# An attention phase that hands its transfers to another engine's queue: half-row tiles, block sums as tasks of their own, and a second bank for the last products

## The chip, the cores and the metric

The kernel runs on one core of a Trainium2 chip. The metric is the device time of one execution in microseconds. Each engine of the core (TensorE, written PE in the profile; VectorE, DVE; ScalarE, ACT; GpSimd, POOL; SyncE, SP) works through its own list of instructions in the order in which the program recorded them, and waits at an instruction until the semaphores that it needs have come. PE's weight loads stand in rows of their own (PEld). SP computes nothing and issues transfers; ACT computes and can issue transfers too. A row whose engine is written SPq or ACTq is such an issue.

## The reference

One decoder layer on x, 2048 rows of 1024 numbers in float32. Three groups of heads share one input projection; their outputs are normalized, projected, and added to x; a feed-forward part with squared ReLU follows.

```python
h = rms_norm(x, norm1_g)
proj = einsum('bld,de->ble', h, w_in)
o_a = swa_sink_mixer(...)      # window attention, 256 columns
o_b = s5_mixer(...)            # state space, 512 columns
o_c = nsa_mixer(...)           # compressed, selected and window attention, 256 columns
mixed = concatenate([rms_norm(o_a, g), rms_norm(o_b, g), rms_norm(o_c, g)])
x = x + einsum('ble,ed->bld', mixed, w_out)
h2 = rms_norm(x, norm2_g)
hid = relu(einsum('bld,df->blf', h2, w_up))
x = x + einsum('blf,fd->bld', hid * hid, w_down)
```

## The kernel before

The rows of x are cut into 16 tiles of 128. A float32 product is made of three products: each operand is split into a high part and the rest (`split`, L1766 and L1767: a cast on ACT, a subtraction on DVE), and high·high, high·low and low·high are summed in one PSUM bank. Phases follow each other: the front (input projection), a stretch that merges window attention, the gated output of the state space and compression, `phase_mix` (about 600 to 1280 us), `phase_up` and `phase_down`.

`phase_mix` holds the third attention, the output projection and the residual. It is written as generators, one for each piece of a tile's work, that yield an engine with an estimated duration, an event, or a ring (a set of buffers). A planner, `Flow`, takes at each step the task that can start first by these estimates, with ties broken by rank, and so fixes one order for each engine when the program is built. On the chip each engine follows that order, whatever the true durations are.

For the output projection of tile i these tasks follow each other:

- `opening`: once for the phase, raw rows of `w_out` are loaded on SP, 128 × 1024 at a time (oraw, L1161), and split into wo_h on ACT (L1168) and wo_l on DVE (L1169).
- `front`: projected queries and keys are loaded on SP (tc, L1192 and L1193).
- `closing`: the attention's output is stored on SP (oc_d, L1579).
- `finished`: the three groups' outputs are loaded on SP (mix, L1595 to L1597) and scaled on POOL (L1604); the third group is squared on ACT (sq, L1608), normalized on POOL (L40 to L45, then L1610). PE transposes (ptx, L1622, in the single bank "pt"), and ACT and DVE split the result into mh (L1624) and ml (L1625), in two halves.
- `filled`: the tile of x is loaded on SP (mx, L1638); then 2 × 24 products (pw, L1657), the first half of the columns before the second, in the single bank "pw". The last tile is an exception: its two halves alternate, and the second uses the bank "pt". Below, pw131 is tile 13's second half.
- `added`: DVE adds pw to mx (L1672), ACT squares the sum into the bank (L1673). Only then is the bank free.
- `posted`: both halves together are stored as x1 on ACT (L1682). For tiles 0 to 7, POOL scales the row (L1689), PE transposes it (pth, L1697), ACT copies (L1701), SP stores it as hT (L1703). At its end, for tiles 7 to 14, one eighth of the block sums is made: four loads of hT on SP (mt, L1715), four subtractions on POOL (L1719), four stores on SP (sums, L1720).

Raw rows of `w_out`, rows of x and block sums share one ring of two 128 × 1024 buffers, "xt". Logits use the two banks of "pq".

`phase_up` multiplies by a scheme of seven products in the order 1, 6, 7, 5, 2, 4, 3. Its factors come from hT (1, 2, 3) and from the block sums (4, 5, 6, 7): each is loaded on SP (fx, L1852) and split into fh (ACT, L1766) and fl (DVE, L1767). The weights' factors are loaded on SP (ur, L1879), partly combined on POOL (fs, L1891), and split into uh and ul. The products (pua to pud) are L1920. Its first loads and splits are recorded among the last work of `phase_mix`.

```python
for i in range(NT):
    spawn(front(i), 100 * i + R_FRONT, 0.0)
    spawn(compressed(i), 100 * i + R_CMP, 0.0)
    spawn(attended(i), 100 * i, 0.0)
    spawn(finished(i), 100 * i + R_FINISH, 0.0)
```

Of the kernel before, what the change touches and what calls it, by code (L numbers as in the profile page):

```python
# [1082 lines left out]
def phase_mix(tc, C, x, gains, B, cmp, w_out, out_norm_g, g2, pd, oa_d, ob, x1, hT, xs, rr, rh, ss_a, ss_b, r_d, oc_d, release):  # L1083
# [4 lines left out]
    with ExitStack() as ctx:  # L1088
# [17 lines left out]
        for t in (kBw[64:96].bitcast(F32), q_lo[0][64:96].bitcast(F32), q_lo[1][64:96].bitcast(F32), slc):  # L1106
# [9 lines left out]
                                     ("qd", 1), ("tc", 1), ("xt", 2), ("mix", 1), ("mh0", 1), ("mh1", 1), ("fill", 1), ("oc", 2))}  # L1116
# [3 lines left out]
        wout = [Event() for _ in range(NK)]  # L1120
# [30 lines left out]
        def opening():  # L1151
# [3 lines left out]
            for k in range(NK):  # L1155
                yield R["xt"]
                box = {}

                def load(k=k):
                    box["r"] = late["fp"].tile([P, D], F32, tag="xt", name=f"oraw{k}", bufs=2)  # L1160
                    nc.sync.dma_start(box["r"], w_out[0, k * P:(k + 1) * P])  # L1161
                t = yield "SP", 50, load
                landed = Event()
                fire(landed, t + DMA_NS + 2600)
                yield landed
                for n in range(2):
                    sl = slice(512 * n, 512 * n + 512)
                    yield "ACT", 714, lambda: nc.scalar.activation(late["wh"][k][:, sl], box["r"][:, sl], AF.Copy, scale=late["go"][:, k:k + 1])  # L1168
                    t = yield "DVE", 796, lambda: nc.vector.scalar_tensor_tensor(late["wl"][k][:, sl], box["r"][:, sl], late["go"][:, k:k + 1],  # L1169
                                                                                 late["wh"][k][:, sl], op0=ALU.mult, op1=ALU.subtract)  # L1170
                put(R["xt"], t)
                fire(wout[k], t)
                if k == 3:
                    yield R["pw"]
                    yield "PE", 60, turn_rows
                    t = yield "DVE", 300, lambda: nc.vector.tensor_copy(late["rb"], late["ptr"])
                    put(R["pw"], t)
# [6 lines left out]
        def front(i):  # L1184
# [5 lines left out]
            def load():  # L1190
                S["tc"] = lp.tile([P, 524], F32, tag="tc", name=f"tc{i}", bufs=1)
                nc.sync.dma_start(S["tc"][:, 0:256], pd["b"][i * P:i * P + P, 128:384])  # L1192
                nc.sync.dma_start(S["tc"][:, 256:524], pd["c"][i * P:i * P + P, 128:396])  # L1193
            t = yield "SP", 100, load
# [365 lines left out]
        def closing(i, exps, fin, den, w, b, po, prev, done, logits_done, nm_, end, rank):  # L1560
# [17 lines left out]
            if end:  # L1578
                t = yield "SP", 50, lambda: nc.sync.dma_start(oc_d[i * P:i * P + P], S["oc"].rearrange("p h d -> p (h d)"))  # L1579
# [3 lines left out]
        def finished(i):  # L1583
# [9 lines left out]
            def load():  # L1593
                mix = box["mix"] = fp.tile([P, D], F32, tag="mix", name=f"mix{i}", bufs=1)
                nc.sync.dma_start(mix[:, 0:256], oa_d[rows])  # L1595
                nc.sync.dma_start(mix[:, 256:768], ob[rows])
                nc.sync.dma_start(mix[:, 768:D], oc_d[rows])  # L1597
            t = yield "SP", 150, load
            yield landing(t, 5e5)
            mix = box["mix"]  # L1600
            if i == 0:
                yield wout[4]
# [29 lines left out]
        def filled(i, mh, ml):  # L1632
            wh, wl = late["wh"], late["wl"]
            yield R["fill"]
            yield R["xt"]
            rows = slice(i * P, i * P + P)
            xt_ = late["fp"].tile([P, D], F32, tag="xt", name=f"mx{i}", bufs=2)
            t = yield "SP", 50, lambda: nc.sync.dma_start(xt_, x[0, rows])  # L1638
            landed, outs = landing(t, 5e5), [Event(), Event()]
            spawn(posted(i, xt_, outs, rows), 100 * i + R_FINISH, 0.0)  # L1640
            order = [(n, k) for n in range(2) for k in range(NK)]
            if i == NT - 1:
                order = [(n, k) for k in range(NK) for n in range(2)]
            pw = {}
            for n, k in order:
                sl = slice(512 * n, 512 * n + 512)
                if i < 2:
                    yield wout[k]
# [661 lines left out]
```

## Time and profile before

| | |
|---|---|
| median of 3 runs | 2544.19 us (2543.75 to 2546.55) |
| profiled execution, its own time | 2548.41 us |
| its span in the trace | 2546.6 us |
| mean granted clock of TensorE in it | 0.984 of full speed |
| PE busy | 96% of the span |
| DVE, ACT, POOL busy | 70%, 52%, 40% |

The span is cut into 40 slices of 63.7 us on the page. Each digit is the busy share of an engine in a slice, in tenths; PEclk is the granted clock. The edited phase holds slices 10 to 20 and the start of 21, counted from 1. How PE's waits lie within these slices is read from the trace's rows: each has its start, its duration, the engine and source line, output and inputs by the program's names, and in brackets the idle time of the engine just before it with what ended that.

### The profile page before, as it was taken

The page shows a single profiled execution, that of the slowest core. Times are in us where ns is not written, and L with a number is a line of the kernel's source. Part 1 is how long each engine was busy: PE and PEld are TensorE (multiplying, and loading weights), DVE is VectorE, ACT ScalarE, POOL GpSimd, SP SyncE. Part 2 cuts the span into 40 slices and gives each one's busy share as a digit, 9 for nine tenths or more (in the row PEclk, how much of TensorE's full clock was granted, in tenths as well). Part 3 has the DMA queues.
Part 4 walks back from the last instruction along what each step waited for, and adds up shares of the span by engine and source line. Part 5 has one row for each costly group of instructions (what it writes and reads, how often), then busy time and mean ns, then how long its engine had stood idle before and what let it go on. Part 6 is the DMA issues. An engine that isn't in the chain of part 4 may idle for free. (4 is left out here: it accounts for less than half of the span.)

```text
span 2546.6 us, 37996 instructions
## 1 busy us (share of the span) xinstructions
PE 2440.5 (96%) x12766; PEld 2071.8 (81%) x12766; DVE 1771.2 (70%) x3496; ACT 1325.9 (52%) x2768; POOL 1021.1 (40%) x1015
## 2 busy tenths in 40 slices
PE   8999998999799999999799999999999999999999
PEld 7799997777578888888578878788887888888887
DVE  7853876754687788888355555755558888888886
ACT  6453546754576667666255554544444444334442
POOL 0000222211243333332646665566555444545447
PEclk9999999999899999999899999999999999999999
DMA  7462335221222122222466667755547534444335
GB/s 234 136 204 83 106 95 169 80 60 42 80 84 84 59 69 75 65 80 77 146 216 186 188 193 220 220 152 153 152 122 262 160 103 125 135 131 132 121 101 196
DMA packets 394867, 337.21 MB, mean 132 GB/s; under 512 B 42758, under 2 KB 357772, under 8 KB 393232
## 3 DMA queue, kind: packets, MB, share of 16 engines
q1 hardware_dynamic: 357488, 308.56, 40.2%
q10 hardware_dynamic: 37184, 26.22, 3.2%
q8 instruction: 101, 1.65, 0.3%
q14 instruction: 94, 0.77, 0.1%
HBM read 220.15 MB, written 114.55 MB: 131 GB/s over the span
## 5 line engine op out<-in xcount | busy, mean ns | idle before, releaser
L1766 ACT CAST v<-vr 128x512 fp32r<-128x512 f32 x224 | 139.4, 624 | 304.7 <-DMA vr<-vd 144.2
L1767 DVE TENSOR_TENSOR v<-vr,v 128x512 fp32r<-128x512 f32 x224 | 233.6, 1051 | 78.8 <-ACT v L1766 78.6
L2099 PE MATMUL pdc<-dw,v 128*128 128x512 f32 x768 | 187.4, 393 | 4.0 <-ACT dw L1766 2.9
L2099 PE MATMUL pdb<-dw,v 128*128 128x512 f32 x768 | 184.7, 389 | 0.0
L2099 PE MATMUL pda<-dw,v 128*128 128x512 f32 x768 | 184.5, 389 | 0.0
L2099 PEld LDWEIGHTS pdc<-dw,v 128*128 128x128 f32 x768 | 145.3, 190 | 35.5 <-ACT dw L1766 3.4
L2099 PEld LDWEIGHTS pdb<-dw,v 128*128 128x128 f32 x768 | 144.5, 188 | 30.1
L2099 PEld LDWEIGHTS pda<-dw,v 128*128 128x128 f32 x768 | 144.1, 188 | 30.0
L546 POOL TENSOR_TENSOR t<-Q,E 128x508 f32<-128x508 f32 x16 | 22.0, 1376 | 362.9 <-ACT Q L526 324.7
L1766 ACT CAST uh<-fs 128x512 fp32r<-128x512 f32 x124 | 76.2, 621 | 157.2 <-PE pub L1920 58.9
L1891 POOL TENSOR_TENSOR fs<-ur,ur 128x512 f32<-128x512 f32 x62 | 87.3, 1408 | 166.6 <-DMA ur<-in_w_up 120.0
L1767 DVE TENSOR_TENSOR ul<-fs,uh 128x512 fp32r<-128x512 f32 x124 | 124.3, 1004 | 35.1 <-ACT uh L1766 34.9
L1767 DVE TENSOR_TENSOR ul<-ur,uh 128x512 fp32r<-128x512 f32 x93 | 93.5, 1007 | 50.1 <-ACT uh L1766 46.8
L1657 PE MATMUL pw<-wo_h,mh 128*128 128x512 f32 x256 | 104.8, 409 | 16.5 <-ACT pw L1673 15.5
L1337 ACT CAST ths<-pps 128x512 fp32r<-128x512 f32 (+1 forms) x144 | 79.0, 563 | 69.8 <-PE pps L1321 62.5
L1936 POOL TENSOR_TENSOR ev<-e,e 128x512 f32<-128x512 f32 x64 | 93.3, 1458 | 49.1 <-issue 24.7
L1920 PE MATMUL puc<-fh,uh 128*128 128x512 f32 x256 | 101.8, 398 | 6.7 <-ACT fh L1766 3.4
L1342 DVE TENSOR_TENSOR tls<-pps,ths 128x512 fp32r<-128x512 f32 (+1 forms) x144 | 92.5, 657 | 21.4 <-ACT ths L1337 20.2
L1920 PE MATMUL pub<-fh,uh 128*128 128x512 f32 x256 | 102.8, 402 | 2.4 <-DVE e L1929 2.4
L1657 PE MATMUL pw<-wo_h,ml 128*128 128x512 f32 x256 | 104.4, 408 | 0.0
L1657 PE MATMUL pw<-wo_l,mh 128*128 128x512 f32 x256 | 104.1, 407 | 0.0
L1920 PE MATMUL pub<-fl,uh 128*128 128x512 f32 x256 | 102.1, 399 | 0.0
(563 smaller groups left out, 7814.7 us busy)
## 6 DMA issues: line engine op xcount, KB each, us to landing
vr<-vd SPq DMA_DIRECT2D x224, 256.0 KB
vd<-ev SPq DMA_DIRECT2D x128, 256.0 KB
ur<-in_w_up SPq DMA_DIRECT2D x124, 256.0 KB
vd<-e ACTq DMA_DIRECT2D x64, 256.0 KB
dr<-in_w_down SPq DMA_DIRECT2D x32, 512.0 KB
x<-in_x SPq DMA_DIRECT2D x16, 512.0 KB
mx<-in_x SPq DMA_DIRECT2D x16, 512.0 KB
x<-mx ACTq DMA_DIRECT2D x16, 512.0 KB
```

The lines of the kernel that those rows point to most:

```text
L546: nc.gpsimd.tensor_tensor(t[:, :, :, 0:n], Q[:, :, :, 0:n], e.rearrange("p g j c -> p j g c")[:, :, :, 0:n], op=ALU.mult)
L1337: yield "ACT", cast_ns(n), lambda: nc.scalar.copy(th[:, 0:nb], pt[:, 0:nb])
L1342: t = yield "DVE", sub_ns(n), lambda: nc.vector.tensor_tensor(tl[:, 0:nb], pt[:, 0:nb], th[:, 0:nb], op=ALU.subtract)
L1657: t = yield "PE", mm_ns(512), lambda: nc.tensor.matmul(pw[n], a[half][:, j], b[k][:, sl], start=k == 0 and m == 0, stop=k == NK - 1 and m ...
L1766: nc.scalar.copy(dh, src)
L1767: nc.vector.tensor_tensor(dl, src, dh, op=ALU.subtract)
L1891: nc.gpsimd.tensor_tensor(t, x, y, op=op)
L1920: nc.tensor.matmul(bank[b], w[:, k], h[o][:, k], start=first and k == 0 and n == 0, stop=k == HALF - 1 and n == 2, skip_group_check=True)
L1936: nc.gpsimd.tensor_tensor(tile_("v" + o), x, y, op=op)
L2099: nc.tensor.matmul(bank[b, q], x[:, q, j], y[:, j], start=first and j == 0 and n == 0, stop=j == 1 and n == 2, skip_group_check=True)
```

## The change

All of it is in `phase_mix`; `phase_up` is as it was, with its line numbers 17 higher.

1. The loads of tc, of raw `w_out`, of mix and of x, and the store of oc_d are issued by ACT instead of SP.
2. The "xt" ring is four buffers of 128 × 512 instead of two of 128 × 1024. Raw rows of `w_out` and rows of x come in halves. x1 is stored half by half. The splitting of a half of the weights is a task of its own (`weighed`), as is the transposition of the norms (`rows_turned`); tiles 0 and 1 wait for each half of a weight row by itself.
3. Block sums are eight tasks of their own (`block_sums`), each started once hT of tiles m and m + 4 is stored, where m is 0 to 3.
4. For tiles 14 and 15 the second half of the products uses a bank of "pq"; tile 15's halves follow each other like the other tiles'.

```diff
-                                     ("qd", 1), ("tc", 1), ("xt", 2), ("mix", 1), ...
+                                     ("qd", 1), ("tc", 1), ("xt", 4), ("mix", 1), ...
-        wout = [Event() for _ in range(NK)]
+        wout = {(k, n): Event() for k in range(NK) for n in range(2)}
+        rows_there = Event()
...
             for k in range(NK):
-                yield R["xt"]
-                    box["r"] = late["fp"].tile([P, D], F32, tag="xt", name=f"oraw{k}", bufs=2)
-                    nc.sync.dma_start(box["r"], w_out[0, k * P:(k + 1) * P])
...
                 for n in range(2):
                     sl = slice(512 * n, 512 * n + 512)
+                    yield R["xt"]
+                    raw = late["fp"].tile([P, 512], F32, tag="xt", name=f"oraw{k}{n}", bufs=4)
+                    t = yield "ACT", 60, lambda: nc.scalar.dma_start(raw, w_out[0, k * P:(k + 1) * P, sl])
+                    spawn(weighed(k, n, raw, sl), 60 + k, t)
                 if k == 3:
+                    spawn(rows_turned(), 60, t)
...
-                nc.sync.dma_start(S["tc"][:, 0:256], pd["b"][i * P:i * P + P, 128:384])
+                nc.scalar.dma_start(S["tc"][:, 0:256], pd["b"][i * P:i * P + P, 128:384])
...
-                t = yield "SP", 50, lambda: nc.sync.dma_start(oc_d[i * P:i * P + P], ...)
+                t = yield "ACT", 60, lambda: nc.scalar.dma_start(oc_d[i * P:i * P + P], ...)
...
-                nc.sync.dma_start(mix[:, 0:256], oa_d[rows])
+                nc.scalar.dma_start(mix[:, 0:256], oa_d[rows])
...
-            order = [(n, k) for n in range(2) for k in range(NK)]
-            if i == NT - 1:
-                order = [(n, k) for k in range(NK) for n in range(2)]
+            spawn(loaded(i, rows, xh, landed), 100 * i + R_FINISH - 2, 0.0)
+            order = [(n, k) for n in range(2) for k in range(NK)]
...
-                    alt = i == NT - 1 and n
-                    yield R["pt"] if alt else R["pw"]
-                    p, tag = (ps_t, "pt") if alt else (late["ps"], "pw")
+                    alt = i >= ENDING and n
+                    yield R["pq"] if alt else R["pw"]
+                    p, tag, bufs = (ps_s, "pq", 2) if alt else (late["ps"], "pw", 1)
...
+        def loaded(i, rows, xh, landed):
+            for n in range(2):
+                yield R["xt"]
+                xh[n] = late["fp"].tile([P, 512], F32, tag="xt", name=f"mx{i}{n}", bufs=4)
+                t = yield "ACT", 60, lambda: nc.scalar.dma_start(xh[n], x[0, rows, 512 * n:512 * n + 512])
...
-            yield "ACT", 60, lambda: nc.scalar.dma_start(x1[rows], xt)
+                t = yield "ACT", 60, lambda: nc.scalar.dma_start(x1[rows, 512 * n:512 * n + 512], xh[n])
...
+        def block_sums(m, half):
+            yield E[m]["hT"]
+            yield E[m + 4]["hT"]
...
+            for m in range(4):
+                for half in range(2):
+                    spawn(block_sums(m, half), 100 * (m + 4) + 450, 0.0)
```

What this moves is seen in the order of the engines' instructions. First ACT at the end of the phase, from the last cast of an up weight (uh0153) on; mh140 and mh141 are the halves of tile 14's transposed rows, pw130 and pw131 the squares that free tile 13's bank. Before:

```order
L1766 CAST uh0153_16049<-fs0154_16043 128x512
L1673 ACTIVATE pw130_15601,xs_15647<-mx13_15590 128x512
L1624 CAST mh140_15683<-ptx140_15685 128x512
L1624 CAST mh141_15709<-ptx141_15711 128x512
L1673 ACTIVATE pw131_15659,xs_15647<-mx13_15590 128x512
L1682 DMA x1_72<-mx13_15590 128x1024
```

The same place of the change:

```order
L1783 CAST uh0153_16129<-fs0154_16123 128x512
L1678 ACTIVATE pw130_15713,xs_15758<-mx130_15700 128x512
L1686 DMA x1_72<-mx130_15700 128x512
L1783 CAST fh06_16135<-fx06_16083 128x2048
L1783 CAST fh07_16141<-fx07_16133 128x2048
L1625 CAST mh140_15791<-ptx140_15793 128x512
L1667 DMA mx140_15815<-in_x 128x512
L1667 DMA mx141_15817<-in_x 128x512
L1625 CAST mh141_15812<-ptx141_15814 128x512
L1678 ACTIVATE pw131_15766,xs_15758<-mx131_15702 128x512
```

The casts of factors 06 and 07, which came after tile 15 before, now stand between the two halves of tile 13, and the loads of tile 14's x stand on ACT. DVE's order follows: fl06 and fl07 ahead of ml140 and of pw131's sum, four ul instead of six ahead of pw130's, and pw121's sum ahead of fl01 instead of behind it.

Second, SP where the phase ends; mt are parts of block sums, fx are factors of the up projection. Before:

```order
L1638 DMA mx14_15721<-in_x 128x1024
L1715 DMA mt13_15741<-hT_74 128x2x128 x4
L1720 DMA sums_75<-mt13_15741 128x2x128 x4
L1638 DMA mx15_15837<-in_x 128x1024
L1715 DMA mt14_15857<-hT_74 128x2x128 x4
L1720 DMA sums_75<-mt14_15857 128x2x128 x4
L1852 DMA fx06_16003<-sums_75 128x2048
L1852 DMA fx07_16053<-sums_75 128x2048
```

The same place of the change:

```order
L1728 DMA mt310_12993<-hT_74 128x2x128 x2
L1728 DMA mt311_13045<-hT_74 128x2x128 x2
L1733 DMA sums_75<-mt310_12993 128x2x128 x2
L1733 DMA sums_75<-mt311_13045 128x2x128 x2
L1869 DMA fx01_16081<-hT_74 128x2048
L1869 DMA fx06_16083<-sums_75 128x2048
L1896 DMA ur01511_16089<-in_w_up 128x4x128
```

The loads of x have left SP, and fx06 follows the last sums ahead of the weights of the up projection; in the order before it followed the last tile's load of x.

Third, ACT in the body, where tile 9's window attention (slw, thw) runs beside tile 6's projection. Before:

```order
L1337 CAST thw904_11408<-ppw904_11379 128x256
L1280 ACTIVATE slw92_11267,denw_11072<-slw92_11267,nmw_11071 128x640
L1280 ACTIVATE slw93_11270,denw_11072<-slw93_11270,nmw_11071 128x640
L1624 CAST mh61_11345<-ptx61_11435 128x512
L1337 CAST thw910_11465<-ppw910_11446 128x512
```

The same place of the change:

```order
L1625 CAST mh61_11391<-ptx61_11416 128x512
L1339 CAST thw904_11459<-ppw904_11429 128x256
L1667 DMA mx60_11420<-in_x 128x512
L1667 DMA mx61_11472<-in_x 128x512
L1597 DMA mix7_11477<-oa_d_71 128x256
L1598 DMA mix7_11477<-ob_70 128x512
L1599 DMA mix7_11477<-oc_d_81 128x256
L1282 ACTIVATE slw92_11349,denw_11067<-slw92_11349,nmw_11066 128x640
```

Five loads now stand between a cast and the exponentials of the same tile. The buffers of mx60 and mx61 have held block sums before, and those two loads wait for the sums' stores. ACT has 244 rows of transfers in the program, before 84.

More of the change, by code (lines that the diff above doesn't have):

```diff
@@ L1179, in landing, with rows_turned @@
+        def rows_turned():
+            yield R["pw"]
+            yield "PE", 60, turn_rows
+            t = yield "DVE", 300, lambda: nc.vector.tensor_copy(late["rb"], late["ptr"])
+            put(R["pw"], t)
+            fire(rows_there, t)
         def landing(t, nbytes):
@@ L1634, in filled @@
             yield R["fill"]
-            yield R["xt"]
             rows = slice(i * P, i * P + P)
[L1637 to L1640, printed above, removed]
+            landed, outs = [Event(), Event()], [Event(), Event()]
+            xh = {}
+            spawn(loaded(i, rows, xh, landed), 100 * i + R_FINISH - 2, 0.0)
+            spawn(posted(i, xh, outs, rows), 100 * i + R_FINISH, 0.0)
             order = [(n, k) for n in range(2) for k in range(NK)]
-            if i == NT - 1:
-                order = [(n, k) for k in range(NK) for n in range(2)]
             pw = {}
@@ L1705, in posted, with turns @@
-            put(R["xt"], t + DMA_NS + 1300)
-            m, ks = (i - 7) // 2, slice(2 * ((i - 7) % 2), 2 * ((i - 7) % 2) + 2)
-            if i < 7 or i == NT - 1:
-                return
-            yield E[7]["hT"]
-            yield R["xt"]
-            t = late["fp"].tile([P, 4, 2, P], F32, tag="xt", name=f"mt{i}", bufs=2)
+            yield "POOL", RSQRT_NS + 200, rsq
+            if i >= NT // 2:
+                return
+            for half in range(2):
+                hx = xh[half].rearrange("p (k t) -> p k t", t=P)
+                yield "POOL", 700, lambda: nc.gpsimd.tensor_scalar(xh[half], xh[half], rr[:, i:i + 1], 1.0, op0=ALU.mult, op1=ALU.mult)
+                yield R["pt"]
+                pt = ps_t.tile([P, 4, P], F32, tag="pt", name=f"pth{i}{half}")
+                def turns():
+                    for j in range(4):
+                        nc.tensor.transpose(pt[:, j], hx[:, j], C["ident"])
+                yield "PE", 4 * TURN_NS, turns
+                for j in range(4):
+                    k = 4 * half + j
+                    t = yield "ACT", 380, lambda: nc.scalar.activation(hx[:, j], pt[:, j], AF.Copy, scale=late["g2"][:, k:k + 1])
+                put(R["pt"], t)
+                t = yield "SP", 50, lambda: nc.sync.dma_start(hT[0, i // 4, half, :, :, i % 4], hx)
+                put(R["xt"], t + DMA_NS)
@@ L1713, in load @@
+            fire(ev["hT"], t + DMA_NS)
+        def block_sums(m, half):
+            yield E[m]["hT"]
+            yield E[m + 4]["hT"]
+            t = []
+            for n in range(2):
+                yield R["xt"]
+                t.append(late["fp"].tile([P, 2, 2, P], F32, tag="xt", name=f"mt{m}{half}{n}", bufs=4))
+            t = [t[n // 2][:, n % 2] for n in range(4)]
+            ks = slice(2 * half, 2 * half + 2)
             def load():
                 for n, (b, k) in enumerate(((0, 0), (1, 0), (1, 1), (0, 1))):
-                    nc.sync.dma_start(t[:, n], hT[0, b, k, :, ks, m])
+                    nc.sync.dma_start(t[n], hT[0, b, k, :, ks, m])
@@ L1737, in starts @@
                     fire(E[i]["go"], 0.0)
+            for m in range(4):
+                for half in range(2):
+                    spawn(block_sums(m, half), 100 * (m + 4) + 450, 0.0)
             spawn(opening(), 60, 0.0)
```

81 lines of the change are left out of this document (30 added, 51 removed).

## The prediction

> **What bounds the kernel now.** I read the page's totals first, then the attention phase cut into stretches, and there the waits of PE.
>
> ```profile
> span 2546.6 us, 37996 instructions
> PE 2440.5 (96%) x12766; PEld 2071.8 (81%) x12766; DVE 1771.2 (70%) x3496; ACT 1325.9 (52%) x2768; POOL 1021.1 (40%) x1015
> ```
>
> PE is idle for 2546.6 − 2440.5 = 106 us. The change removes no matmul, so it can win only from that, and from matmuls that run slow. The windows say which part the edited phase holds:
>
> ```profile
> core 0: us, PE busy (x) PEld busy (x) DVE busy (x) ACT busy (x) POOL busy (x), PEclk, DMA share, GB/s
> 660.00:760.00 100.00, 87.86 (x534) 73.77 (x535) 85.05 (x261) 74.49 (x210) 37.76 (x66) 0.93 0.30 94
> 760.00:1220.00 460.00, 451.27 (x2976) 398.24 (x2975) 368.01 (x1062) 302.69 (x714) 157.03 (x338) 1.00 0.24 74
> 1220.00:1280.00 60.00, 42.59 (x178) 33.29 (x177) 15.00 (x22) 12.76 (x28) 40.33 (x71) 0.89 0.46 141
> 1280.00:1300.00 20.00, 14.15 (x54) 10.81 (x53) 9.93 (x9) 10.61 (x13) 4.99 (x11) 0.83 0.73 244
> ```
>
> From 760 to 1220 (the body) PE lacks only 8.7 us of 460: whatever is done to its transfers has at most that to win. The first 100 us lack 12.1, with DVE at 85% and ACT at 74%. The last 60 us lack 17.4, with every vector engine slack, and the first 20 us of the up projection 5.9. So the gain, if there is one, lies in the 80 us from 1220 on. PE's waits from 1220 to 1300 (us, times, longest) and the rows behind them:
>
> ```profile
> PE pw L1657 <- ACT pw L1673: 15.3, 4, 6.1
> PE puc L1920 <- ACT fh L1766: 3.4, 1, 3.4
> PE pud L1920 <- ACT fh L1766: 2.4, 1, 2.4
> ```
>
> ```profile
> 1225.36 0.51 PE L1657 MATMUL pw<-wo_h,mh 128*128 128x512 f32 x1 [2.89 <-ACT pw L1673]
> 1237.18 0.79 PE L1657 MATMUL pw<-wo_h,mh 128*128 128x512 f32 x1 [6.09 <-ACT pw L1673]
> 1246.95 0.50 PE L1657 MATMUL pw<-wo_h,mh 128*128 128x512 f32 x1 [1.29 <-ACT pw L1673]
> 1257.71 0.79 PE L1657 MATMUL pw<-wo_h,mh 128*128 128x512 f32 x1 [5.02 <-ACT pw L1673]
> 1258.30 0.63 PE L1657 MATMUL pw<-wo_l,mh 128*128 128x512 f32 x1
> 1261.65 0.39 PE L1657 MATMUL pw<-wo_h,mh 128*128 128x512 f32 x1
> 1269.15 0.50 PE L1657 MATMUL pw<-wo_h,mh 128*128 128x512 f32 x1 [0.71 <-DVE ml L1625]
> 1284.81 0.50 PE L1920 MATMUL pud<-fh,uh 128*128 128x512 f32 x1 [2.42 <-ACT fh L1766]
> 1288.74 0.80 PE L1920 MATMUL puc<-fh,uh 128*128 128x512 f32 x1 [3.42 <-ACT fh L1766]
> 1292.31 0.40 PE L1920 MATMUL pud<-fh,ul 128*128 128x512 f32 x1
> 1295.73 0.39 PE L1920 MATMUL pua<-fh,uh 128*128 128x512 f32 x1
> ```
>
> The bank "pw" is single: pw131, pw140 and pw141 (tile and half) each start when ACT has squared the half before. After the two long waits a matmul starts every 0.43 us for about nine rows, then every 0.23 (1292.31 to 1295.73 is 15 starts, 0.228 each). So 1257.71 to 1261.65 costs nine starts' excess, 3.94 − 9 × 0.228 = 1.9 us beyond its wait, and 1288.74 to 1292.31 likewise 3.57 − 8 × 0.228 = 1.7.
>
> **The change, part by part.** The sum is made against the profiled execution, 2548.41 us: 2546.6 of span and 1.8 around it. That is 4.2 above the median of the three runs, 2544.19.
>
> *Second bank.* pw141 takes a "pq" bank, idle by then since the last logits are done. Its 5.02 us of wait and 1.9 of slow starts go. pw151 moves out of the transposes' bank too, where pw15 waited 0.71 for ml151. Against this, pw150 needs pw140's square; pw141's 24 matmuls (24 × 0.228 = 5.5 us) cover its add and square, if mx140 has landed. That load is what made the old wait:
>
> ```profile
> 1242.93 0.59 ACT L1624 CAST mh<-ptx 128x512 fp32r<-128x512 f32 x1 [5.80 <-PE ptx L1622]
> 1251.50 0.33 SPq L1638 DMA_DIRECT2D mx<-in_x  x1
> 1256.16 0.69 DVE L1672 TENSOR_TENSOR mx<-mx,pw 128x512 f32<-128x512 f32 x1 [9.16 <-DMA mt<-hT]
> ```
>
> The add of pw140 ran right as the load landed, 4.7 us after issue; the releaser that the row names was a transfer, only not this one. In the new order mx140 stands right behind mh140 on ACT, which is the row at 1242.93, so it is issued at about 1243.6 and lands by 1248.3; pw140's last product is due at 1246.95 + 5.5 = 1252.4. This part is −7.6, from −8 if all goes to −5 if pw150 still waits; I take **−7.5**.
>
> *Waits ahead of it, pw130 to pw140.* pw130 waits for pw121's add, which stood behind fl:
>
> ```profile
> 1219.70 1.92 ACT L1766 CAST fh<-fx 128x2048 fp32r<-128x2048 f32 x1
> 1221.67 2.28 DVE L1767 TENSOR_TENSOR fl<-fx,fh 128x2048 fp32r<-128x2048 f32 x1
> 1221.84 2.70 POOL L1399 TENSOR_TENSOR oc<-oc,otw 128x256 f32<-128x256 f32 x1 [2.25 <-DVE otw L1392]
> 1225.72 0.74 POOL L1399 TENSOR_TENSOR oc<-oc,otw 128x256 f32<-128x256 f32 x1
> ```
>
> The add now stands ahead of fl (2.28), but its square still follows fh and mh131 on ACT: pw130 starts some 1.5 earlier. pw131's add stands behind four ul instead of six, worth perhaps 0.8 at its start. Then comes what is given back: with block sums stored early, factors 06 and 07 are cast here, two fh of 1.9 on ACT and two fl of 2.3 on DVE, ahead of mh140, ml140 and pw131's add and square. Besides, while fl ran, POOL's add took 2.70 against 0.74, so each fl may hold tile 14's normalization on POOL by 2.0, and PE's transpose ptx140 stands within pw131's matmuls. If the fl's finish while PE is at pw131, pw140 starts 1.3 earlier; if they come in the way of both, 2.5 later. I take **+0.5**, near the middle, as no row shows where fx06 lands.
>
> *Start of the up projection.* The factor loads and casts that PE waits for:
>
> ```profile
> 1274.59 2.80 SPq L1720 DMA_DIRECT2D sums<-mt  x4
> 1278.09 0.81 SPq L1852 DMA_DIRECT2D fx<-sums  x2
> 1282.86 1.90 ACT L1766 CAST fh<-fx 128x2048 fp32r<-128x2048 f32 x1 [1.69 <-DMA fx<-sums]
> 1286.79 1.90 ACT L1766 CAST fh<-fx 128x2048 fp32r<-128x2048 f32 x1 [2.03 <-DMA fx<-sums]
> ```
>
> The last block sums leave SP at 1277.4, hence the factors come late. The new order has the sums stored, loaded and cast before tile 14 is done. 2.42 + 3.42 + 1.7 = 7.5 go. The next factors, 05 and 04, are late next: fh05's buffer is free only after pw151's last matmul, and 04 follows fl05. Two casts (1.9), two subtractions (2.3) and a load (4.7) are 13.1 us, beside which PE works off the factors 06 and 07. The old waits of 2.42 and 3.42 were those of a factor that comes late by one cast and one subtraction; one such wait may return, 1.9 + 2.3 = 4.2 at most. Between −7.5 and −3.3, I take **−6**: nearer to none, since two factors are on hand where before there was one.
>
> *Beginning of the phase.* Half-row loads let the weights start on half the bytes, and tile 0's product stands 115 PE rows earlier; but DVE is the engine here, and its work is the same, the 16 weight subtractions of 0.744 (11.9 us) among it:
>
> ```profile
> 661.20 0.69 PE L1321 MATMUL ppc<-c_ident,slc 128*128 128x128 f32 x2 [7.96 <-DVE tls L1342]
> L1169 DVE SCALAR_TENSOR_TENSOR wo_l<-oraw,wo_g,wo_h x16: 734/744/1107, 667.5 to 739.3; 128x512 fp32r<-128x512 f32 x16
> ```
>
> The reordering puts seven DVE instructions that prepare tile 1 behind the norm chain, where they had filled its pauses; at the mean of the window, 85.05/261 = 0.33, they are 2.3 us, ahead of the row at 661.20 that already waits 7.96 for DVE. An earlier pw00 can fill some of the 12.1 us of idle PE, but by tile 7 the orders have met, so I give it a quarter, 3. From −3 to +5 (twice those 2.3); I take **+2**, since DVE is the bound here.
>
> *The body.* 160 more issues stand on ACT. A row of before shows one beside a busy ACT, and SP's rows show what they cost one after another:
>
> ```profile
> 749.89 0.61 ACT L1673 ACTIVATE pw<-mx 128x512 f32<-128x512 f32 x1
> 750.07 0.36 ACTq L1682 DMA_DIRECT2D x<-mx  x1
> 1249.74 0.54 SPq L1595 DMA_DIRECT2D mix<-oa_d  x1
> ```
>
> The issue at 750.07 lies inside the square and costs nothing. Three loads of mix end 1.8 us after 1249.74 (mx follows at 1251.50), of which one compute row of 0.6 hides a third. Twelve tiles × 1.2 = 14 us on ACT, which is 66% busy here, so PE sees a part: between 0 and 14. What the loads wait for is the larger question. On SP it was free; on ACT everything behind stands still:
>
> ```profile
> SPq L1579 <- POOL oc L1399: 141.7, 15, 22.2
> SPq L1595 <- PE ptx L1622: 128.6, 11, 28.1
> SPq L1638 <- DMA sums<-mt: 8.8, 8, 2.2
> ```
>
> The written order puts these issues on ACT later than they stood on SP, behind work that follows their releasers, so most of these 280 us are not carried over. The mx loads are the exception: their buffers now pass through block sums, so mx60 to mx81 wait for stores of sums with thw and slw behind them; six loads × at most 2.2 is 13. On the gaining side the body has 8.7 us in all, and no row speaks for a part of it. I take **+3** of 0 to 14, near the hidden end, since pw products stand ready for PE in the body (8.7 idle of 460).
>
> Sum: −7.5 + 0.5 − 6 + 2 + 3 = **−8**: 2540.4 profiled, 2536 as a median.
>
> The Trainium skill, page "DMA: Bandwidth & Descriptors", section "Issuing engines are not separate DMA queues", says that issuing from several engines saves sequencer time only. By it the move to ACT would be worth at most SP's issue time and could not speed a transfer; the trace agrees so far that the DMA share of the body is 0.24.
>
> **Rivals.**
> *Bigger gain.* Products that start earlier fill the 12.1 us of 660 to 760, and the factor chain costs nothing: −7.5 − 1.3 − 7.5 − 3 = −19 at most, 2525 as a median. For it: the weights are ready earlier in the order. Against: DVE at 85%.
> *Given back.* pw140 comes 2.5 later, pw150 waits, factor 04 is 4 late, the start costs 4: −5 + 2.5 − 3.5 + 4 + 3 = +1, 2540 to 2549. This also stands for a change that does not do what it says: the wait at pw141 leaves and returns at pw140.
> *Slower.* ACT's queue is held at loads that wait for buffers or for POOL's oc, in the body, where ths and thw casts release PE within microseconds. The other terms sum to −11, used up when 12 tiles lose 0.9 us each; from 1.3 each it is slower by over 0.2%, at 1.5 each +7 (2551), at the longest hold of 2.2 each +15 (2559). For it: every hold on ACT stands ahead of casts that PE's next products need. Against: ACT's slack of a third. The Trainium skill, page "Perfetto Trace Analysis", section "DMA Instruction — HWDGE (DVE, Sync)", shows a DMA instruction waiting for its semaphores in the sequencer, ahead of what follows; SP's waits above agree, no ACT issue of this trace can.
>
> **How the numbers follow.** Forecast (2530 to 2540) 0.45; bigger gain 0.13; given back 0.23; slower 0.19. The forecast's own range is 2530 to 2540. The range that is to hold eight in ten goes from 2524 to 2552: it leaves out the outer part of the slower case. 0.2% (5.1 us) is about what a measurement of this kernel can tell from no change: faster is under 2539.1, so the forecast counts almost whole and the bigger gain whole, 0.56; slower is above 2549.3, 0.19; the rest is 0.25.
>
> **What would show it.** In the tail PE's wait for ACT at pw141 is gone and pw150 follows pw141 within 1 us; otherwise term one is wrong. The first puc and pud rows start without a wait of over 1 us; if 05 or 04 waits over 4, term three is. Windows of 760 to 1220 cut by tile show PE at 98%; if it falls below 96%, look at ACT's queue for loads with waits, and the slower case has come. PE's idle time ahead of tile 2 tells the start. The forecast falls if PE's idle time from 1220 on stays over 15 us.

## The result, and the profile after

| | before | changed |
|---|---|---|
| median | 2543.97 us of 4 runs (2543.35 to 2546.55) | 2521.52 us of 4 runs (2519.97 to 2523.44) |
| ratio, 95% interval | | 0.991 (0.9893 to 0.9927) |
| profiled execution, own time | 2548.41 us | 2519.97 us |
| span | 2546.6 us | 2518.2 us |

The change gains 22.5 us in the medians, 28.4 between the two profiled executions (that of before lies 4.4 above its median, that of the change 1.5 below). 8 were forecast, and 2524 was the range's lower end.

The page's totals of the changed kernel, span and busy time by engine:

```profile
span 2518.2 us, 38031 instructions
PE 2426.2 (96%) x12766; PEld 2067.3 (82%) x12766; DVE 1786.7 (71%) x3496; ACT 1328.5 (53%) x2768; POOL 1030.8 (41%) x1023
```

The same stretches as before, in the same columns:

```profile
660.00:760.00 100.00, 88.10 (x552) 77.70 (x551) 84.87 (x253) 76.79 (x217) 40.57 (x74) 0.90 0.27 85
760.00:1220.00 460.00, 449.89 (x2986) 398.31 (x2985) 370.89 (x1066) 307.04 (x711) 173.86 (x360) 1.00 0.28 87
1220.00:1280.00 60.00, 49.75 (x207) 39.60 (x208) 27.26 (x28) 24.96 (x39) 40.27 (x62) 0.91 0.47 159
1280.00:1300.00 20.00, 19.84 (x85) 15.86 (x86) 16.18 (x16) 11.51 (x19) 10.83 (x8) 1.00 0.61 179
```

By busy time alone the start and the body look as they did. But a stretch of fixed time holds other work now, so landmarks are needed: rows that mean the same work in both. These are PE's waits at the end of the attention phase in the changed kernel:

```profile
1212.60 0.50 PE L1655 MATMUL pw<-wo_h,mh 128*128 128x512 f32 x1 [1.29 <-ACT pw L1678]
1224.88 0.80 PE L1655 MATMUL pw<-wo_h,mh 128*128 128x512 f32 x1 [6.54 <-ACT pw L1678]
1233.99 0.44 PE L1623 MATMUL ptx<-c_ident,mix 128*128 128x128 f32 x2 [0.93 <-POOL mix L1611]
1235.73 0.79 PE L1655 MATMUL pw<-wo_h,mh 128*128 128x512 f32 x1 [1.30 <-ACT pw L1678]
1250.24 0.66 PE L1623 MATMUL ptx<-c_ident,mix 128*128 128x128 f32 x4 [1.40 <-DVE ml L1626]
1263.34 0.50 PE L1937 MATMUL pua<-fh,uh 128*128 128x512 f32 x1 [1.53 <-ACT pw L1678]
```

pw130 starts at 1212.60, before at 1225.36: 12.8 us are won ahead of the tail. The first product of the up projection starts at 1263.34, before at 1279.49 (the first pua in the listing of PE): 16.2, so the tail wins 3.4. The tile pua then shows its first and last start, first of the kernel before, then of the change:

```profile
L1920 PE MATMUL pua<-fh,uh x256: 389/395/397, 1279.5 to 1918.9; 128*128 128x512 f32 x128
```

```profile
L1937 PE MATMUL pua<-fh,uh x256: 389/395/500, 1263.3 to 1889.5; 128*128 128x512 f32 x128
```

639.4 us against 626.2: another 13.2 in the up projection, whose code was not edited. Some 3 of these belong to this one execution of the kernel before: in the four other kernels with late block sums (below) the first and the last pua lie 634.1 to 636.2 us apart, in the nine profiled executions with early ones, the change's among them, 624.3 to 628.8. About 10 is the up projection's share. In these two profiles 12.8 + 3.4 + 13.2 = 29.4, of which 1.0 is given back later. The forecast had these three as +3.5 (beginning +2, body +3, pw130's own −1.5), −5.5 and −6.

The 12.8 lie where the weights of `w_out` are made: tile 2's first product starts at 768.57, before at 782.59, so the lead is 14.0 there, and about 1.3 of it are lost up to pw130. The tile views of oraw, of the kernel before and then of the change (minimum, median and maximum in ns, first and last start):

```profile
L1161 SPq DMA_DIRECT2D oraw<-in_w_out x8: 328/376/429, 661.6 to 730.1; - x8
```

```profile
L1161 ACTq DMA_DIRECT2D oraw<-in_w_out x16: 334/335/456, 647.9 to 684.0; - x16
L1169 DVE SCALAR_TENSOR_TENSOR wo_l<-oraw,wo_g,wo_h x16: 735/744/1450, 661.5 to 690.5; 128x512 fp32r<-128x512 f32 x16
```

The last subtraction of a weight starts at 739.3 before, and at 690.5 now. Three things in the change could do that: the queue, the casts as tasks of their own, or the four half buffers. The experiments take them apart first.

### The profile page after: what moved, and what is told of

Its sections match the earlier page's. It is cut to its first block, busy times and chain, and to the rows that moved or that the text cites. A ratio compares the mean times of both kernels' runs of the same rounds, so it can differ in the third digit from the quotient of the medians.

```text
span 2518.2 us, 38031 instructions
## 1 busy us (share of the span) xinstructions
PE 2426.2 (96%) x12766; PEld 2067.3 (82%) x12766; DVE 1786.7 (71%) x3496; ACT 1328.5 (53%) x2768; POOL 1030.8 (41%) x1023
## 5 line engine op out<-in xcount | busy, mean ns | idle before, releaser
L1784 DVE TENSOR_TENSOR ul<-fs,uh 128x512 fp32r<-128x512 f32 x124 | 132.3, 1069 | 28.5 <-ACT uh L1783 28.0
L1784 DVE TENSOR_TENSOR ul<-ur,uh 128x512 fp32r<-128x512 f32 x93 | 98.6, 1061 | 45.0 <-ACT uh L1783 41.5
L1655 PE MATMUL pw<-wo_h,mh 128*128 128x512 f32 x256 | 106.4, 416 | 10.4 <-ACT pw L1678 10.2
L1937 PE MATMUL pua<-fh,uh 128*128 128x512 f32 x256 | 100.8, 394 | 1.5 <-ACT pw L1678 1.5
```

The lines of the kernel that those rows point to most:

```text
L1655: t = yield "PE", mm_ns(512), lambda: nc.tensor.matmul(pw[n], a[half][:, j], b[k][:, sl], start=k == 0 and m == 0, stop=k == NK - 1 and m ...
L1784: nc.vector.tensor_tensor(dl, src, dh, op=ALU.subtract)
L1937: nc.tensor.matmul(bank[b], w[:, k], h[o][:, k], start=first and k == 0 and n == 0, stop=k == HALF - 1 and n == 2, skip_group_check=True)
```

## The experiments

Each comparison gives the median of its runs, and beside it that of the kernel before measured along with it, with the ratio and its 95% interval. The kernel before took 2541.97 to 2544.59 in these series of runs, so a difference between medians of two series can be off by some 2.6 us; the ratios take this out.

### The queue: all transfers back on SP

Here for the loads of mix; those of tc, w_out and x and the store of oc_d are changed alike.

```diff
-                nc.scalar.dma_start(mix[:, 0:256], oa_d[rows])
+                nc.sync.dma_start(mix[:, 0:256], oa_d[rows])
...
-            t = yield "ACT", 180, load
+            t = yield "SP", 150, load
```

> The change with all its moved transfers back on SP's queue (tc, w_out, mix, x, oc_d), the halves, tasks, sums and bank kept. Theory Q: the 12 us that are gained before tile 13 come of the queue, since on SP the loads of w_out and of the next tile's tc stand behind stores that wait for an attention result (in before the last raw row was issued at 730.1, in the change at 684.0). Then 10 to 12 us are lost, 2531 to 2534. Theory H: they come of four half buffers and of casts that are tasks of their own, whatever the queue. Then nothing or under 3 us is lost, 2521 to 2524, and the last raw row still goes out before 700.

Measured: 2518.75 against 2541.97, ratio 0.991 (0.9894 to 0.9926). It is as fast as the change, and the first product of the up projection starts at 1264.47. The tile view of oraw has the last raw row going out at 687.9:

```profile
L1161 SPq DMA_DIRECT2D oraw<-in_w_out x16: 327/330/424, 660.3 to 687.9; - x16
```

Theory Q falls: 160 transfers on ACT instead of SP bring nothing and cost nothing that these runs can tell, once the casts are tasks of their own.

The rival "slower" had priced such transfers on ACT at up to 15 us. The place in the body whose order is shown further up, in the trace of the change:

```profile
911.93 0.37 ACT L1339 CAST thw<-ppw 128x256 fp32r<-128x256 f32 x1
912.07 0.82 ACTq L1667 DMA_DIRECT2D mx<-in_x  x2
912.92 0.45 ACTq L1597 DMA_DIRECT2D mix<-oa_d  x1
914.38 0.83 ACT L1282 ACTIVATE slw<-slw,nmw 128x640 f32<-128x640 f32 x1 [2.08 <-DMA mx<-in_x]
```

ACT does stand still, 2.08 us, for five issues in a row. That is the length of the issues: the two of mx go out while the cast before them still runs, so they did not have to wait for the stores of block sums here. From 760 to 1200 us no issue on ACT begins more than 0.53 us after the row before it ended. So the queue was not held in the body, and from 760 to 1220 PE lacks 10.1 us where it lacked 8.7.

### The weights: casts in the loading task again

```diff
-                    spawn(weighed(k, n, raw, sl), 60 + k, t)
+                    yield from weighed(k, n, raw, sl)
```

> The change with the casts of each half row of w_out written into the loading task again, so that the next half is asked for only after the one before is split; queue, halves, sums and bank are kept. Theory H: the weights become late again, the first product pw00 moves from 698 to beyond 715, and 8 us or more are lost, 2529 to 2533. Theory Q: the queue alone brings the weights early enough, under 3 us are lost, 2521 to 2525.

Measured: 2537.04 against 2541.97, ratio 0.9976 (0.9966 to 0.9986): 15.5 above the change's median. pw00 starts at 729.3, the last raw half goes out at 766.4. Theory H stands, but this overshoots, since sixteen halves in series take longer than eight rows. The fairer form loads both halves of a row and then splits both:

```diff
+                raws = []
                 for n in range(2):
...
-                    spawn(weighed(k, n, raw, sl), 60 + k, t)
+                    raws.append(late["fp"].tile([P, 512], F32, tag="xt", name=f"oraw{k}{n}", bufs=4))
+                    t = yield "ACT", 60, lambda: nc.scalar.dma_start(raws[n], w_out[0, k * P:(k + 1) * P, sl])
+                for n in range(2):
+                    yield from weighed(k, n, raws[n], slice(512 * n, 512 * n + 512))
```

> The change with w_out loaded and split row by row as in the kernel before: both halves of a row are loaded, then both split, and only then the next row is asked for. The half rows alone in series lost 15 us, but they paid 16 round trips where the kernel before pays 8. Theory H (casts in the loading task make each row wait for the one before): the last raw row goes out at about 730 as in before, and 8 to 12 us are lost, 2529 to 2533. If the loss of 15 came of the 16 round trips alone, under 3 us are lost.

Measured: 2527.29 against 2542.98, ratio 0.9935 (0.9917 to 0.9954), 5.8 above the change's median and 7.1 above that of its repetition in the same series (below). This is a little under the 8 to 12 expected and over the 3 of the other reading. pw00 starts at 723.6. But the last raw half goes out at 753.7 and not at about 730: on ACT's queue the serial rows come later than in the kernel before, so this is not quite that kernel's splitting either. The next experiment is free of this.

### The weights' tasks alone, in the kernel before

```diff
-                landed = Event()
-                fire(landed, t + DMA_NS + 2600)
-                yield landed
-                for n in range(2):
-                    sl = slice(512 * n, 512 * n + 512)
-                    yield "ACT", 714, lambda: nc.scalar.activation(late["wh"][k][:, sl], box["r"][:, sl], ...)
-                    t = yield "DVE", 796, lambda: nc.vector.scalar_tensor_tensor(late["wl"][k][:, sl], ...)
-                put(R["xt"], t)
-                fire(wout[k], t)
+                spawn(weighed(k, box["r"], t), 60 + k, t)
```

The removed lines are the new task `weighed`. As in the change, the transposition of the norms becomes a task too, and all tiles wait for it.

> The kernel before with one edit: the casts of each row of w_out are a task of their own, so that the loading goes on; whole rows, two buffers, SP's queue, block sums and banks stay as they were. Theory H: the weights are ready 30 us earlier or more, and 8 to 12 us are gained, 2530 to 2535. If four half buffers or the queue are needed as well, because loads of w_out still stand behind stores that wait on SP and behind two buffers, 0 to 4 us are gained, 2538 to 2543.

Measured: 2536.32 against 2542.98, ratio 0.9971 (0.996 to 0.9982): 6.7 us from this edit alone, with whole rows, two buffers and SP's queue. That lies between the two ranges expected. The tile view of oraw:

```profile
L1162 SPq DMA_DIRECT2D oraw<-in_w_out x8: 332/336/422, 661.9 to 691.6; - x8
L1175 DVE SCALAR_TENSOR_TENSOR wo_l<-oraw,wo_g,wo_h x16: 737/744/1218, 667.7 to 700.7; 128x512 fp32r<-128x512 f32 x16
```

The first load goes out at the same time as before (661.9, before 661.6), the last 38.5 us earlier. So neither SP's queue nor two buffers forbid early weights; the order does. In the planner's times the load of row k + 1 came after the last subtraction of row k, and so the loads, casts and subtractions were spread among the attention's work in the orders of SP, ACT and DVE. On the chip a load waits for its place in that order and for its buffer, not for the subtraction as such: in the kernel before the second load goes out at 662.96, ahead of the first cast at 666.51, but later ones stand right behind a store that waits for an attention result:

```profile
686.45 0.32 SPq L1579 DMA_DIRECT2D oc_d<-oc  x1
686.82 0.43 SPq L1161 DMA_DIRECT2D oraw<-in_w_out  x1
710.04 0.32 SPq L1579 DMA_DIRECT2D oc_d<-oc  x1
710.46 0.38 SPq L1161 DMA_DIRECT2D oraw<-in_w_out  x1
```

With the tasks the loads stand in pairs, and the second pair goes out ahead of the first store of oc_d:

```profile
671.05 1.00 SPq L1162 DMA_DIRECT2D oraw<-in_w_out  x2
676.12 0.33 SPq L1587 DMA_DIRECT2D oc_d<-oc  x1
```

What PE does with it is seen in windows of 700 to 920 us, of the kernel before:

```profile
700.00:760.00 60.00, 55.30 (x353) 46.23 (x353) 50.11 (x147) 44.20 (x119) 23.97 (x50) 0.99 0.27 86
760.00:840.00 80.00, 77.98 (x515) 68.45 (x514) 57.48 (x168) 52.64 (x146) 31.44 (x68) 1.00 0.22 69
840.00:920.00 80.00, 77.81 (x494) 68.04 (x493) 58.59 (x184) 50.14 (x130) 25.98 (x58) 0.98 0.20 63
```

and of this kernel:

```profile
700.00:760.00 60.00, 58.14 (x391) 51.66 (x391) 49.37 (x157) 45.24 (x132) 23.24 (x48) 1.00 0.25 80
760.00:840.00 80.00, 78.85 (x529) 70.24 (x528) 58.19 (x169) 54.04 (x145) 29.85 (x65) 1.00 0.21 70
840.00:920.00 80.00, 78.78 (x528) 69.35 (x527) 64.91 (x204) 54.94 (x138) 29.29 (x65) 1.00 0.21 66
```

PE's idle time of these 220 us falls from 8.9 to 4.2, its clock is full throughout, and 1448 matmuls run where 1362 did. From 640 to 700 us it is the other way, 204 matmuls against 228, so the net gain is read from landmarks: tile 2's first product starts 6.9 us earlier than before (775.74 against 782.59), tile 6's 9.0 (915.16 against 924.18), and tile 13's again 9.0 (1216.40 against 1225.36). Once the weights are split, the projection's products are work that PE can do at any time, and they fill the gaps of the attention, up to tile 6 and not only while the weights are made.

### Block sums: late again, and early alone

```diff
-            yield E[m]["hT"]
-            yield E[m + 4]["hT"]
+            yield E[7]["hT"]
+            yield E[7 + 2 * m + half]["po"]
```

The event "po" of a tile is fired where `posted` ends.

> The change with block sums tied to the end of tiles 7 to 14 again, as before, the rest kept. If the early factors are worth the forecast's third term (7.5 us less what is late next), this is slower than the change by 6 to 8 us, 2528 to 2530, with PE waits of 2.4 and 3.4 us for fh back at the start of the up projection. If the changed kernel's 12 us between the first up product and the end come of something else in the up projection (waits for DVE's sums at 1423 and 1485 in the profile of before), it is slower by those 7.5 only; if early sums caused these waits to go as well, by 12.

Measured: 2531.72 against 2541.97, ratio 0.9957 (0.9945 to 0.997): 10.2 above the change's median. The first 31 us from the first product of the up projection on, in the windows of this kernel, of the kernel before and of the change:

```profile
1269.00:1300.00 31.00, 25.29 (x93) 19.31 (x92) 21.92 (x17) 18.27 (x20) 11.71 (x12) 0.89 0.76 251
```

```profile
1279.00:1310.00 31.00, 25.14 (x100) 19.33 (x100) 18.59 (x16) 17.86 (x21) 8.22 (x12) 0.89 0.79 255
```

```profile
1263.00:1294.00 31.00, 30.30 (x130) 24.18 (x131) 23.49 (x21) 20.19 (x27) 17.35 (x15) 1.00 0.54 170
```

37 matmuls fewer than in the change, and 37 × 0.228 = 8.4 us. PE waits 1.90, 1.83 and 1.83 for fh and fl there, and runs at 0.89 of its clock; the change has neither. The waits for DVE in the middle of the up projection of before, the longest of them this row,

```profile
1485.58 0.50 PE L1920 MATMUL puc<-fh,uh 128*128 128x512 f32 x1 [2.03 <-DVE eu L1929]
```

are not in this kernel, so they do not follow from late sums alone. But they come only with them: the kernel before, the tasks alone, the bank alone and the halves alone, all with late sums, each have a wait for DVE's eu of 0.8 us or more (2.0 at most) between 1356 and 1486 us, and none of the nine profiles with early sums has one. How the late factors lead to them is not shown. From first to last pua it takes 635.0 us, between the change's 626.2 and the 639.4 of before.

The kernel before, with early sums alone:

```diff
-            if i < 7 or i == NT - 1:
-                return
-            yield E[7]["hT"]
+        def block_sums(m, half):
+            yield E[m]["hT"]
+            yield E[m + 4]["hT"]
             yield R["xt"]
```

> The kernel before with one edit: block sums are tasks of their own as in the change; whole rows, SP's queue, the serial splitting of w_out and the single bank stay. Taking the early sums out of the change cost it 10 us. If the parts add, 8 to 10 us are gained here, 2533 to 2536, and the waits for fh at the first pud and puc and those for DVE at 1362 to 1485 are gone. If the early factors only pay because the second bank or the halves clear the tail for them, under 4 us are gained, since the forecast's price (casts of factors ahead of tile 14) is paid here too.

Measured: 2533.3 against 2544.59, ratio 0.9954 (0.9937 to 0.9972), 11.3 us. From the first to the last pua it takes 624.3 us (1273.2 to 1897.5). The profiled execution is the fastest of five (2527.28 to 2538.78), so its own times flatter this kernel; by the median and its interval the early sums pay by themselves and in full. Their price shows too, at pw131, which waited 6.09 before:

```profile
1235.54 0.80 PE L1657 MATMUL pw<-wo_h,mh 128*128 128x512 f32 x1 [8.81 <-ACT pw L1673]
```

### The second bank: taken out, alone, and for one half more

```diff
-                    alt = i >= ENDING and n
-                    yield R["pq"] if alt else R["pw"]
+                    alt = i == NT - 1 and n
+                    yield R["pt"] if alt else R["pw"]
```

> The change without its second bank: all halves of tiles 0 to 14 use the single bank pw, and tile 15's halves alternate as before with the second in the transposes' bank. If the bank is worth what the forecast's first term says (7.5 us: the 5.0 us wait and nine slow starts at pw141), this runs at about 2529. If the wait only moves to the other halves (the changed kernel still waits 6.54 at pw131 and gained no more than 3.4 us between pw130 and the first up product), it runs at 2523 to 2526.

Measured: 2524.65 against 2541.97, ratio 0.9939 (0.9918 to 0.996): 3.1 above the change's median. In its listing of PE pw141 waits again:

```profile
1247.84 0.80 PE L1657 MATMUL pw<-wo_h,mh 128*128 128x512 f32 x1 [6.28 <-ACT pw L1680]
```

The first product of the up projection starts at 1269.52, 6.2 later than in the change. The medians and the profiles differ by the scatter of single runs (2522.77 to 2532.35 here), so the bank's worth in the change is 3 to 7: 3 by the medians, 6 by the profiles, 7 by the ratios (0.9939 and 0.991), whose intervals overlap.

The same edit alone in the kernel before:

> The kernel before with one edit: the second halves of tiles 14 and 15 use the bank of the logits, and tile 15's halves follow each other. The forecast priced this at 7.5 us; taking it out of the change cost 3 in the median and 6 at the first up product of the profile. If the factors then are simply waited for (they follow the last block sums, which do not move), 0 to 3 us are gained, 2540 to 2543; if the bank pays by itself, 5 to 7, 2536 to 2538.

Measured: 2542.13 against 2544.59, ratio 0.9992 (0.9981 to 1.0003), which is no difference that is sure. PE's waits at the first products, in its trace:

```profile
1275.98 0.50 PE L1918 MATMUL pua<-fh,uh 128*128 128x512 f32 x1 [1.53 <-ACT pw L1671]
1281.64 0.50 PE L1918 MATMUL pud<-fh,uh 128*128 128x512 f32 x1 [2.65 <-ACT fh L1764]
1285.44 0.80 PE L1918 MATMUL puc<-fh,uh 128*128 128x512 f32 x1 [3.31 <-ACT fh L1764]
```

The wait at pw141 is gone, and pua comes 3.5 earlier; the transposes of tile 15 wait 1.70 and 1.00 in its place, and the factors still hold pud and puc by 6.0.

With all transfers on SP, tile 13's second half was given the second bank as well:

```diff
-                    alt = i >= ENDING and n
+                    alt = i >= ENDING - 1 and n
```

> The kernel with all transfers back on SP and, besides, tile 13's second half in the second bank too. If the single bank is what holds PE at pw131 (6.5 us of wait and two of slow starts in the change, 1.6 in the kernel on SP's queue), up to 3 us are gained here. If tile 14's normalization on POOL is next in the chain (the transposes of tile 14 wait 3.7 us for it there), the wait moves to them and nothing is gained, 2517 to 2520.

Measured: 2522.37 against 2542.98, ratio 0.9913 (0.9897 to 0.993), no better than without it. In its trace PE no longer waits at pw131, but at the transposes of tile 14:

```profile
1231.71 0.69 PE L1623 MATMUL ptx<-c_ident,mix 128*128 128x128 f32 x2 [2.75 <-DVE ml L1626]
1237.31 0.69 PE L1623 MATMUL ptx<-c_ident,mix 128*128 128x128 f32 x2 [4.91 <-POOL mix L1611]
```

Behind the bank stands tile 14's normalization on POOL, as expected; one wait took the place of the others (without the edit PE waits 1.60 at pw131, and 1.10 and 3.66 at these transposes).

### Do the parts add? Three without the halves, the halves without the three

The kernel before with the tasks, the early sums and the bank (the three edits shown above), still with whole rows in two buffers, on SP:

> The kernel before with three edits: splitting of w_out as tasks, block sums as tasks, the second bank; still whole rows in two buffers and all transfers on SP. If queue and halves are worth nothing, this is as fast as the change, 2518 to 2524. If the four half buffers are needed for the parts to work together, it is slower by 3 us or more, 2525 to 2531.

Measured: 2530.0 against 2544.59, ratio 0.9943 (0.9927 to 0.996), 14.6 us and not 22. The parts alone gave 6.7, 11.3 and 2.5, 20.5 together. By the ratios and their intervals that is 21 ± 6 against 14.5 ± 4 (an estimate, the intervals added as squares), so that it is likely but not certain that the parts give less together. A place where this kernel falls behind the one with halves on SP is the tail, in ACT's rows:

```profile
1230.99 0.62 ACT L1775 CAST uh<-fs 128x512 fp32r<-128x512 f32 x1 [4.64 <-POOL fs L1900]
1231.52 1.90 ACT L1775 CAST fh<-fx 128x2048 fp32r<-128x2048 f32 x1
1233.32 0.59 ACT L1678 ACTIVATE pw<-mx 128x512 f32<-128x512 f32 x1
```

pw130's square, which frees the bank, stands behind a cast that waits 4.64 for POOL and behind a factor's cast of 1.90, and pw131 waits 10.46:

```profile
1234.09 0.80 PE L1662 MATMUL pw<-wo_h,mh 128*128 128x512 f32 x1 [10.46 <-ACT pw L1678]
```

In the kernel with halves on SP that square stands ahead of both, pw131 waits 1.60 and starts at 1224.38, here at 1234.09, and the first up product at 1264.47 against 1270.90. So with the halves the tail's work stands in another order. That they bring this about by freeing buffers earlier is a guess that was not tried. Nor is the tail the whole of it: of the 9.7 us between the spans of the two profiles, 4.5 are there at pw130 already (1217.87 against 1213.42), 1.9 come up to the first up product, as most of what is lost at pw131 is made up again, and 2.9 in the up projection (628.8 against 625.9).

The halves alone, on SP, with serial rows, late sums and the single bank:

> The half rows alone: the change with its transfers back on SP, w_out split row by row in the loading task, block sums tied to the ends of tiles 7 to 14, and the single bank; what is left of it are halves of x, of w_out and of x1 in four buffers. The other three edits together gained 14.6 us where the whole change gains 22 to 25, so that the halves carry 8 to 11 in company. If they pay by themselves (smaller transfers land sooner, a half is given back sooner), 6 to 11 us are gained, 2533 to 2538. If they pay only in company, because they leave buffers for block sums and weights to run ahead, it is 2541 to 2545.

Measured: 2547.15 against 2544.23, ratio 1.0009 (0.9997 to 1.0021). Alone they gain nothing.

### The change again

> The changed kernel as it is, as an anchor beside the others of this call. If its gain of 22 us over the kernel before stands, it runs at 2518 to 2524. If the kernel with all transfers back on SP is really the faster of the two, this lies above that one's 2518.75 by 2 us or more; if the queue decides nothing, within 2.

Measured: 2520.22 against 2542.98, ratio 0.9906 (0.9886 to 0.9925). The gain stands, and the kernel on SP's queue, at 2518.75, is within 2 us: no version here beats the change beyond the scatter.

## Why the prediction was wrong

**The direction was right, the size was not.** −8 was forecast, −22.5 came. By the landmarks of the profiles, the step that failed is the *beginning of the phase*. It said that "DVE is the engine here, and its work is the same", and took +2. DVE's work is the same indeed: the 16 subtractions have the same median of 0.744 us. The inference from it was wrong: not the amount of DVE's work but its place in the order was the limit. The products of the first tiles wait for the weights row by row, and the last subtraction started at 739.3 where it could start at 700.7 with the tasks alone. The rows that said so were at hand: the eight raw loads were spread over 661.6 to 730.1. The prediction quoted the subtraction's spread, 667.5 to 739.3, and read only its sum, 11.9 us, out of it. By the tasks alone this step is −6.7 (0.996 to 0.9982; −9.0 by the landmarks of the profiles), by taking them out of the change row by row −6 to −7. That is 9 to 11 of the 14.5 us by which the forecast was off.

The rival "bigger gain" had this mechanism and gave it 3 us, a quarter of the 12.1 us that PE is idle from 660 to 760. The quarter was the wrong size, and the place too: the gain comes up to 920 us, as idle time, as clock, and as denser matmuls within time that counts as busy.

**The start of the up projection** was right in kind and too small: −6 was forecast, −7.5 at most. Removed from the change, the early sums are worth 10.2, alone 11.3. The new wait for factors 05 and 04, for which 1.5 was taken off, did not come; behind its first product the change has no wait over 0.3 us in the first 330 us of the up projection. And the old cost was over the two waits that were counted, as the 31 us windows show: 100 to 130 matmuls by the kernel before and the change, 6.8 us, and some more later on, of which the waits for DVE at 1423 and 1485 are a part.

**The second bank** was right at its place and too large in sum: −7.5 was forecast, 3 to 7 are lost without it, and alone it gives nothing sure. The wait of 5.02 at pw141 is gone, but the first up product now waits 1.53 for a square, and tile 14's start came later.

**Waits ahead of it** were right: pw130's wait fell by 1.6 (1.5 was said), ptx140 waits for POOL's mix (0.93), and from pw130 to pw140 it takes 23.1 where it took 21.6. That is +1.5; with pw130's own 1.6 the term is −0.1, inside −1.3 to +2.5.

**The body** was forecast at +3 and rival "slower" at up to +15. It is near nothing: PE lacks 10.1 us instead of 8.7, and from tile 2's first product to tile 13's it takes 444.03 us where it took 442.77. The sentence of the Trainium skill, page "DMA: Bandwidth & Descriptors", section "Issuing engines are not separate DMA queues", agrees with the runs: 2518.75 on SP, 2520.22 and 2521.52 on ACT. The Trainium skill, page "Perfetto Trace Analysis", section "DMA Instruction — HWDGE (DVE, Sync)", shows a DMA instruction waiting for its semaphores in the sequencer; one place on ACT fits it, at the end of the phase, where an issue begins 4.7 us after the one ahead of it ended:

```profile
1235.44 0.47 ACTq L1598 DMA_DIRECT2D mix<-ob  x1
1240.64 0.33 ACTq L1599 DMA_DIRECT2D mix<-oc_d  x1
```

In the body, which the rival was about, there is no such gap.

**What stays open** is the halves. With the other three edits they are worth 11 us by the medians (2518.75 against 2530.0, in two series) and 8 by the ratios (0.991 and 0.9943 of some 2543), alone nothing. The traces show three places of it, 4.5 us ahead of tile 13, 1.9 in the tail and 2.9 in the up projection; why the halves bring these was not taken apart.

## What to carry to other kernels

When an operand is prepared once for a whole phase, look at the spread between its first and last piece, not at the sum of the work: if a loading task splits what it loads before it asks for the next piece, the planner spreads the pieces among other work, and the second buffer did not prevent it here. A task for each piece gained 6.7 us. Price such a delay by what could have run on the bound engine, to the end of the stretch where it has gaps, and not by a share of that engine's idle time beside the delay. And the worth of a part can hang on the others where a planner places them: an edit that gained nothing alone was worth some 8 to 11 with the rest.

## What the runs showed of the hardware

That a long DVE subtraction slows POOL was in the prediction (2.70 against 0.74). How much it slows the shortest instructions was not expected. This row of POOL, in the trace of the change, works on a single column; DVE's two fl run from 1226.65 on, for 4.49 us together:

```profile
1226.86 2.13 POOL L41 TENSOR_SCALAR nr<-nqh 128x1 int32<-128x1 int32 x1
```

The same instruction of the same chain, in the trace of before, with no fl beside it:

```profile
1237.07 0.19 POOL L41 TENSOR_SCALAR nr<-nqh 128x1 int32<-128x1 int32 x1
```

In the trace of the change this instruction runs 16 times, once for each tile, with a median of 0.19; in the trace of before none of the 16 took over 0.20. 2.13 is about the 2.25 of one fl: POOL's tiny step lasted as long as the subtraction that it met. The next step met the second fl, and took 2.26 where its median is 0.34:

```profile
1229.11 2.26 POOL L44 TENSOR_SCALAR nqt<-nr,nqh 128x1 f32<-128x1 f32 x1
```

The normalization of a tile is a chain of eight such steps, so one that meets a few long subtractions is held by their length and not by its own work. The Trainium skill, page "GPSIMD Engine Reference", section "Key points", names contention of POOL with DVE instructions that have two inputs in SBUF, which fl is; the rows agree with it and give the size.
